# Layer 0's differential attention: the second score product over all 128 rows, with k's halves copied by DMA, and a head's closing transposes one iteration later

## The chip, the cores and the metric

The kernel runs on one core of a Trainium2 chip. The metric is the device time of one execution in microseconds. Differences are judged on repeated executions of both kernels; the profile is one execution of its own.

## The reference

Two encoder layers over 512 tokens of width 1024 are computed in float32. Each layer applies a token mixer, then cross-attention into 256 memory tokens, then a gated MLP, each followed by a layer norm. The mixer of layer 0 is the part that matters here, differential attention with 8 heads. A head has two query and key components of 64 numbers and one value of 128:

```python
s = jnp.einsum('bqhce,bkhce->bhcqk', q_blk, k) * (E ** -0.5)
s = s - slopes[None, :, None, None, None] * dist[None, None, None]
p = jax.nn.softmax(s, axis=-1)
attn = p[:, :, 0] - lam_full * p[:, :, 1]
return jnp.einsum('bhqk,bkhe->bqhe', attn.astype(v.dtype), v)
...
o = rms_norm(o, subln) * (1.0 - lambda_init)
return o.reshape(B, S, D) @ w_o
```

## The kernel before

Almost all matrix products take both operands as a sum of a high and a low part, each in the format float32r: hi is a cast of the number, lo is the rest. `mm3` (lines 238 to 245) issues three products of 512 columns, hi*hi, hi*lo and lo*hi (lines 239, 240, 241), into one PSUM bank. TensorE's order is written out by hand. The orders of the other engines come from a scheduler.

**The heads loop of layer 0** (`diff_attention`, from line 496). `proj(h)` computes a head's q, then its k, each by 24 products into one bank of 128 rows: component 0 in rows 0 to 63, component 1 in rows 64 to 127. `stack_q` (line 468) makes two tiles of 128 rows, q0 with component 0's hi in rows 0 to 63 and its lo in rows 64 to 127, q1 with component 1's hi in rows 64 to 127 and its lo in rows 0 to 63. `stack_k` (line 477) makes k0 and k1, with a component's hi in both halves of the rows, and one tile kl with the lo of component 0 in rows 0 to 63 and that of component 1 in rows 64 to 127. It takes four casts of 64 rows on ScalarE (lines 480, 481, 484, 485) and two subtractions on VectorE (482, 483).

`scores(h, q)` (line 552) handles 128 queries and 512 keys. `stacked_scores` (line 487) issues four products into two banks: a 128-row product for each component, which gives q_hi*k_hi + q_lo*k_hi (line 490), and then for each component a product over 64 rows alone, which adds q_hi*k_lo (line 493). VectorE adds the distance table and takes the extreme (line 561), ScalarE takes the exponential (563), VectorE joins the two components (566 to 568). `turn` (571) transposes the result with four products (574), and ScalarE copies it (576). `values` (579) multiplies by V (582) and normalises: a square on ScalarE (585), a small step on VectorE (586), a power on GpSimd (588, the tile rr), and the tile `on` on VectorE (589, 590). `close` (592) transposes a head's four pieces of `on` (595) and splits them into hi and lo.

`main` (600) runs these as a pipeline over n = 32 iterations, four to a head, and LAG + 2 = 4 more. Iteration i issues scores of i, turn of i - 2, values of i - 3, and behind the values of every fourth iteration the close of the head whose last values came one iteration before. It yields a position ahead of each step. `weave` (287) fills the time up to that position with the products of the next head's `proj`, at head 2 with `vproj1` as well, and at the end with the first output products (`early`). In the additional iterations `take(late, 1900)` issues more output products. `proj(0)` runs ahead of the loop, and then 0.4 of `proj(1)` stands ahead of the first scores.

POOL (GpSimd) issues nothing in the loop but the power of line 588. It issues DMAs of its own in layer 1 alone (line 764 among them, the loads of F). The weights come by SP's queue (line 181), and are split by ScalarE and VectorE (218, 219).

## Time and profile before

| | |
|---|---|
| Three executions | 1897.64, 1899.86, 1900.0 us, median 1899.86 |
| The profiled execution, its own time | 1899.72 us |
| Span of the profile (first to last instruction) | 1897.9 us |
| Granted TensorE clock, mean | 0.998 |
| Busy: TensorE, VectorE, ScalarE, GpSimd | 1871.9, 952.9, 763.3, 73.0 us |
| First and last score product of layer 0 | 45.5 and 223.6 us |

Engines are PE (TensorE's products), PEld (its weight loads, which overlap products), DVE (VectorE), ACT (ScalarE), POOL (GpSimd) and SP (SyncE, which issues DMAs). L490 is line 490 of the kernel. Products are pipelined, so the durations of neighbours overlap, and the distance of two starts says what one costs. A wait's row names the waiting instruction and what released it; "issue" means that nothing in the profile held it. A group's row ends with busy time and mean duration, a timeline's row begins with start and duration.

### The profile page before, as it was taken

Reading aid. Unit: us, or ns where it says so; the run is one execution under the profiler, and the core shown is the slowest. Engines: PE = TensorE matmul, PEld = TensorE weight load, DVE = VectorE, ACT = ScalarE, POOL = GpSimd, SP = SyncE. Lnnn points to the kernel's source line nnn. Section 1 sums busy time; section 2 is a strip of 40 time slices with the busy share of each in tenths; the row PEclk is TensorE's granted clock in tenths of the full one; section 3 lists DMA queues with packets and bytes.
Section 4 is the critical chain, followed back from the end, with each engine's and each line's share of the span. In section 5 each row is a group of like instructions: output and inputs, shape, how many; then the busy total and the mean of one; then the engine's idle time right before and its main releaser. Section 6 shows DMA issues by size and latency. Waiting matters only on the chain.

```text
span 1897.9 us, 25004 instructions
## 1 busy us (share of the span) xinstructions
PE 1871.9 (99%) x9896; PEld 1574.6 (83%) x9896; DVE 952.9 (50%) x1761; ACT 763.3 (40%) x1372; POOL 73.0 (4%) x116
## 2 busy tenths in 40 slices
PE   9999999999999999999999999998999999999998
PEld 7777788889888888898898898987888898888886
DVE  5588675557444432533444344444855564444324
ACT  4567654325333321324434344343544243333211
POOL 0001110000000000000000000001000000000000
PEclk9999999999999999999999999999999999999999
DMA  6121066234332334332322232221651352333241
GB/s 237 45 78 56 23 219 191 67 118 150 100 97 93 100 100 151 104 120 100 97 77 84 78 101 87 80 80 46 224 189 65 122 157 90 99 100 96 93 144 45
DMA packets 61573, 204.35 MB, mean 108 GB/s; under 512 B 8080, under 2 KB 8720, under 8 KB 61456
## 3 DMA queue, kind: packets, MB, share of 16 engines
q1 hardware_dynamic: 46080, 165.89, 27.5%
q10 hardware_dynamic: 12816, 32.47, 4.7%
q0 software_dynamic: 2560, 4.39, 1.0%
q8 instruction: 78, 1.28, 0.3%
q14 instruction: 39, 0.32, 0.1%
HBM read 190.01 MB, written 12.71 MB: 107 GB/s over the span
## 4 chain that ended last, share of the span: by engine, by line
PE 92%; DVE 4%; DMA 2%; ACT 1%; issue 1%; POOL 0%; DVEq 0%; POOLq 0%; ACTq 0%; SPq 0%
PE ps_a L239 17%; PE ps_a L240 16%; PE ps_a L241 16%; PE ps_o L239 7%; PE ps_o L241 7%; PE ps_o L240 7%; PE ps_s L241 2%; PE ps_s L240 2%; PE ps_s L239 2%; PE ps_t L239 2%; PE ps_t L241 2%; PE ps_t L240 2%; PE S L716 1%; PE ps_t L785 1%; PE ps_t L770 1%; PE ps_o L582 1%
## 5 line engine op out<-in xcount | busy, mean ns | idle before, releaser
L219 DVE TENSOR_TENSOR wlo<-raw,whi 128x1024 fp32r<-128x1024 f32 (+1 forms) x309 | 376.7, 1220 | 454.5 <-ACT whi L218 449.3
L218 ACT CAST whi<-raw 128x1024 fp32r<-128x1024 f32 (+1 forms) x309 | 323.6, 1049 | 574.3 <-PE ps_a L240 277.6
L239 PE MATMUL ps_a<-x2h,whi 128*128 128x512 f32 (+1 forms) x384 | 152.4, 397 | 0.0
L241 PE MATMUL ps_a<-x2h,wlo 128*128 128x512 f32 (+1 forms) x384 | 146.6, 382 | 0.0
L240 PE MATMUL ps_a<-x2l,whi 128*128 128x512 f32 (+1 forms) x384 | 146.2, 381 | 0.0
L239 PE MATMUL ps_a<-whi,x2h 128*128 128x512 f32 (+1 forms) x256 | 90.2, 352 | 0.0
L725 DVE CUSTOM_DVE_ANT_0 u<-S,tabd 128x256 f32<-128x256 f32 x128 | 48.8, 420 | 79.0 <-PE ps_t L770 78.2
L240 PE MATMUL ps_a<-wlo,x2h 128*128 128x512 f32 (+1 forms) x256 | 87.1, 340 | 0.0
L241 PE MATMUL ps_a<-whi,x2l 128*128 128x512 f32 (+1 forms) x256 | 87.1, 340 | 0.0
L241 PEld LDWEIGHTS ps_a<-x2h,wlo 128*128 128x128 f32 x384 | 72.2, 188 | 14.5
L239 PEld LDWEIGHTS ps_a<-x2h,whi 128*128 128x128 f32 x384 | 72.3, 188 | 14.3 <-issue 1.5
L727 ACT ACTIVATE u<-u,st 128x256 f32<-128x256 f32 x128 | 64.0, 502 | 47.2 <-DVE st L725 47.0
L240 PEld LDWEIGHTS ps_a<-x2l,whi 128*128 128x128 f32 x384 | 72.5, 189 | 11.6
L239 PE MATMUL ps_o<-x1h,whi 128*128 128x512 f32 (+1 forms) x192 | 71.6, 373 | 0.0
L239 PE MATMUL ps_o<-x4h,whi 128*128 128x512 f32 (+1 forms) x192 | 71.6, 373 | 0.0
L240 PE MATMUL ps_a<-x4l,whi 128*128 128x512 f32 (+1 forms) x192 | 71.3, 372 | 0.0
L239 PE MATMUL ps_a<-x1h,whi 128*128 128x512 f32 (+1 forms) x192 | 71.3, 372 | 0.0
L240 PE MATMUL ps_a<-x1l,whi 128*128 128x512 f32 (+1 forms) x192 | 71.3, 372 | 0.0
L239 PE MATMUL ps_a<-x4h,whi 128*128 128x512 f32 (+1 forms) x192 | 71.3, 371 | 0.0
L241 PE MATMUL ps_a<-x4h,wlo 128*128 128x512 f32 (+1 forms) x192 | 71.3, 371 | 0.0
L241 PE MATMUL ps_a<-x1h,wlo 128*128 128x512 f32 (+1 forms) x192 | 71.3, 371 | 0.0
L241 PE MATMUL ps_o<-x1h,wlo 128*128 128x512 f32 (+1 forms) x192 | 71.3, 371 | 0.0
(420 smaller groups left out, 4487.5 us busy)
## 6 DMA issues: line engine op xcount, KB each, us to landing
raw<-in_wall_dram SPq DMA_DIRECT2D x314, 512.0 KB, 3.5
y<-row ACTq DMA_DIRECT2D x40, 256.0 KB, 3.0
row<-y ACTq DMA_DIRECT2D x20, 512.0 KB, 5.4
row<-in_lngb_dram ACTq DMA_DIRECT2D x12, 512.0 KB, 4.6
F<-fd POOLq DMA_DIRECT2D x16, 256.0 KB, 4.3
row<-in_x_dram ACTq DMA_DIRECT2D x4, 512.0 KB, 6.5
out_dram<-row ACTq DMA_DIRECT2D x8, 256.0 KB, 2.1
raw<-in_wall_dram ACTq DMA_DIRECT2D x2, 256.0 KB, 4.4
```

Source lines behind the costliest of these rows:

```text
L218: nc.scalar.copy(hi, ps)
L219: nc.vector.tensor_tensor(lo, ps, hi.bitcast(F32), op=ALU.subtract)
L239: nc.tensor.matmul(ps, ah, bh, start=start, stop=False)
L240: nc.tensor.matmul(ps, ah, bl, start=False, stop=False)
L241: nc.tensor.matmul(ps, al, bh, start=False, stop=stop)
L582: nc.tensor.matmul(o, PT[:, k, :], V[:, k, sl(h)], start=k == 0, stop=k == 3)
L716: nc.tensor.matmul(Ss[b, c][:, f], q_[h, b, :], k_[h], start=True, stop=True)
L725: nc.vector.tensor_tensor_reduce(out=u[:, f], in0=S[:, f], in1=t, scale=-slope, scalar=3.0e38, op0=ALU.add, op1=ALU.min, accum_out=m)
L727: nc.scalar.activation(u[:, f], u[:, f], AF.Exp, bias=m, scale=-1.0, accum_out=s[:, b, 2 * c + 1:2 * c + 2])
L770: nc.tensor.transpose(tp[:, k, :], u[:, sl(k)], ident)
L785: nc.tensor.matmul(o[sl(c, 64), sl(2 * (n // 2) + x)], V[:, :64], PTs[2 * x + c][:, n, :], start=n % 2 == 0, stop=n % 2 == 1)
```

## The change

Each of k0 and k1 becomes a tile of 128 rows, two planes and 512 columns: a component's hi in plane 0 and its lo in plane 1, both in both halves of the rows. A component's own half is filled by a cast on ScalarE and a subtraction on VectorE, and the other half by one DMA of 64 rows x 4 KB on GpSimd's queue. The tile kl is gone. The second score product of a component takes plane 1 over all 128 rows, so that q_lo*k_lo is added as well, and the four products come component by component. The close of a head moves from the iteration after its last values to the one after that, the loop has one more iteration, and the positions in the last head's stretch are divided accordingly.

```diff
-    def stack_k(ps, k0, k1, kl):
+    def stack_k(ps, k0, k1):
 
         a, b = slice(0, 64), slice(64, 128)
-        nc.scalar.copy(k0[a, :], ps[a, :])
-        nc.scalar.copy(k1[b, :], ps[b, :])
-        nc.vector.tensor_tensor(kl[a, :], ps[a, :], k0[a, :].bitcast(F32), op=ALU.subtract)
-        nc.vector.tensor_tensor(kl[b, :], ps[b, :], k1[b, :].bitcast(F32), op=ALU.subtract)
-        nc.scalar.copy(k0[b, :], ps[a, :])
-        nc.scalar.copy(k1[a, :], ps[b, :])
-
-    def stacked_scores(Ss, t, qs, ks, kl):
-
-        for c, S in enumerate(Ss):
-            nc.tensor.matmul(S, qs[c][:, t], ks[c], start=True, stop=False)
-        for c, S in enumerate(Ss):
-            h = sl(c, 64)
-            nc.tensor.matmul(S, qs[c][h, t], kl[h, :], start=False, stop=True)
+        for k, h, o in ((k0, a, b), (k1, b, a)):
+            nc.scalar.copy(k[h, 0, :], ps[h, :])
+            nc.vector.tensor_tensor(k[h, 1, :], ps[h, :], k[h, 0, :].bitcast(F32), op=ALU.subtract)
+            nc.gpsimd.dma_start(k[o], k[h])
...
-            k = [ap.tile([128, 512], F32R, tag=f"k{c}", name="k") for c in range(3)]
+            k = [ap.tile([128, 2, 512], F32R, tag=f"k{c}", name="k") for c in range(2)]
             stack_k(ps, *k)
-            qk[h] = q, k[:2], k[2]
+            qk[h] = q, k
...
-            stacked_scores(Ss, sl(q), *qk[h])
+            for c, (qc, kc) in enumerate(zip(*qk[h])):
+                for n in range(2):
+                    nc.tensor.matmul(Ss[c], qc[:, sl(q)], kc[:, n, :], start=n == 0, stop=n == 1)
...
-            for i in range(n + LAG + 2):
+            for i in range(n + LAG + 3):
                 seg = min(i // 4, DH - 1)
-                base = (i - 4 * seg) / (4.0 if seg < DH - 1 else LAG + 5.0)
-                step = 1.0 / 12 if seg < DH - 1 else 1.0 / (3 * LAG + 15)
+                base = (i - 4 * seg) / (4.0 if seg < DH - 1 else LAG + 6.0)
+                step = 1.0 / 12 if seg < DH - 1 else 1.0 / (3 * LAG + 18)
...
-                j = i - LAG - 2
+                j = i - LAG - 3
                 if 0 <= j < n and j % 4 == 3:
                     close(j // 4, on.pop(j // 4))
```

In the changed kernel the lines behind `stack_k` have other numbers: the casts are L481, the subtractions L482, the copies L483, the score products L549, turn's products L566, those of values L574 and those of close L587.

TensorE, around the first scores of head 3, before. The values of iteration 11 (L582) are followed by the close of head 1 (L595), a filling product of each kind and the scores (L490, L493):

```order
L582 MATMUL ps_o<-V,PT 128x128 x4
L595 MATMUL ps_t<-ident,on 128x128 x4
L239 MATMUL ps_a<-xh,whi_642 128x512
L240 MATMUL ps_a<-xl,whi_642 128x512
L241 MATMUL ps_a<-xh,wlo_643 128x512
L490 MATMUL ps_s<-k,q 128x512 x2
L493 MATMUL ps_s<-k,q 128x512 x2
```

The same place after. The scores of head 3 (L549, four in one form) follow the values (L574) by three filling products, and the close (L587) stands behind the values of iteration 12:

```order
L574 MATMUL ps_o<-V,PT 128x128 x4
L239 MATMUL ps_a<-xh,whi_639 128x512
L240 MATMUL ps_a<-xl,whi_639 128x512
L241 MATMUL ps_a<-xh,wlo_640 128x512
L549 MATMUL ps_s<-k,q 128x512 x4
```

```order
L574 MATMUL ps_o<-V,PT 128x128 x4
L587 MATMUL ps_t<-ident,on 128x128 x4
L239 MATMUL ps_a<-xh,whi_645 128x512
L240 MATMUL ps_a<-xl,whi_645 128x512
L241 MATMUL ps_a<-xh,wlo_646 128x512
```

So the close has gone from in front of a head's first scores to behind them.

VectorE at head 7's k, before. The names are u and m (scores evacuated, their extreme) and ss (the small step of values); k_2058 is kl:

```order
L568 SCALAR_TENSOR_TENSOR u_2034<-u_2038,rc_2042,u_2034 128x512
L561 ISA u_2099,m_2100<-ps_s_2093,tabf_103 128x512
L561 ISA m_2100 128x1
L482 TENSOR_TENSOR k_2058<-ps_a_1947,k_2056 64x512
L483 TENSOR_TENSOR k_2058<-ps_a_1947,k_2057 64x512
L586 TENSOR_SCALAR ss_2082<-ss_2082 128x1
```

After, k_2049 is k0 and k_2050 is k1:

```order
L560 SCALAR_TENSOR_TENSOR u_2027<-u_2031,rc_2035,u_2027 128x512
L482 TENSOR_TENSOR k_2049<-ps_a_1933,k_2049 64x512
L578 TENSOR_SCALAR ss_2074<-ss_2074 128x1
L553 ISA u_2091,m_2092<-ps_s_2085,tabf_103 128x512
L553 ISA m_2092 128x1
L482 TENSOR_TENSOR k_2050<-ps_a_1933,k_2050 64x512
```

The two subtractions are no longer neighbours: a small step and a score evacuation stand between them. Heads 3 and 5 have the same order.

GpSimd at head 3's k, after. Before, only the powers (rr) stood here:

```order
L580 TENSOR_TENSOR rr_995<-ss_992,mhalf_75 128x1
L580 TENSOR_TENSOR rr_1053<-ss_1050,mhalf_75 128x1
L483 DMA k_1089<-k_1089 64x1024
L483 DMA k_1090<-k_1090 64x1024
L580 TENSOR_TENSOR rr_1119<-ss_1116,mhalf_75 128x1
```

Each copy waits for its component's subtraction, and the next power stands behind both copies.

## The prediction

> **What bounds the kernel now.** I read the page, then the stretch of layer 0's attention, its waits, and the timeline around single score products.

> ```profile
> span 1897.9 us, 25004 instructions
> PE 1871.9 (99%) x9896; PEld 1574.6 (83%) x9896; DVE 952.9 (50%) x1761; ACT 763.3 (40%) x1372; POOL 73.0 (4%) x116
> PE 92%; DVE 4%; DMA 2%; ACT 1%; issue 1%; POOL 0%; DVEq 0%; POOLq 0%; ACTq 0%; SPq 0%
> ```

> ```profile
> 120.00:206.00 86.00, 86.00 (x473) 67.00 (x472) 70.43 (x189) 62.63 (x151) 8.77 (x16) 1.00 0.16 50
> ```

> TensorE is busy for 99% of the span and carries 92% of the chain. In 86 us of the heads loop (second view: PE, PEld, DVE, ACT, POOL, then clock and DMA share) it never rests; VectorE has 70.43 us of work and ScalarE 62.63. So time is won here only by a shorter sequence of TensorE instructions, and every wait put on TensorE is lost in full. DMA has room (0.16).

> The waits of the stretch from 36 to 262 us (engine, line, tile, released by, us in total, times, longest):

> ```profile
> PEld ps_s L493 <- issue: 11.4, 32, 0.4
> PEld ps_a L239 <- issue: 7.2, 30, 0.2
> ...
> PEld ps_s L490 <- DVE m L561: 1.2, 3, 0.5
> ...
> PEld ps_t L595 <- DVE on L590: 0.5, 1, 0.5
> PEld ps_s L490 <- ACT k L485: 0.3, 1, 0.3
> ```

> The two large rows are the weight loader, not held by any engine: once per iteration ahead of the 64-row product (L493), and nearly once per iteration ahead of the first projection product behind it. What TensorE itself loses by that is in the timeline (start, duration):

> ```profile
> 82.65 0.40 PE L241 MATMUL ps_a<-whi,xl 128*128 128x512 f32 x1
> 82.88 0.62 PE L490 MATMUL ps_s<-k,q 128*128 128x512 f32 x2
> 83.43 0.50 PE L493 MATMUL ps_s<-k,q 64*128 64x512 f32 x2
> 83.86 0.50 PE L239 MATMUL ps_a<-whi,xh 128*128 128x512 f32 x1
> 84.19 0.40 PE L240 MATMUL ps_a<-wlo,xh 128*128 128x512 f32 x1
> 84.43 0.40 PE L241 MATMUL ps_a<-whi,xl 128*128 128x512 f32 x1
> ```

> Starts are the measure, since durations overlap. A 128-row product of 512 columns takes 0.23 us from start to start (82.65 to 82.88), entering the scores costs nothing, but the two 128-row products take 0.55 instead of 0.46, the 64-row pair 0.43, and the next projection product 0.33.

> ```profile
> L490 PE MATMUL ps_s<-k,q x64: 387/396/502, 45.5 to 223.1; 128*128 128x512 f32 x64
> L493 PE MATMUL ps_s<-k,q x64: 491/493/501, 46.2 to 223.6; 64*128 64x512 f32 x64
> ```

> One 64-row product lasts 0.49 us, and the pair together 0.50: the two halves of the array run side by side.

> **Scores, 32 iterations.** Before: 82.88 to 84.19, 1.31 us, for four score products and one projection product. After: five 128-row products of one form, 5 x 0.23 = 1.15. That is 0.16 less per iteration, 32 x 0.16 = 5.1 us, all on TensorE's path. The count of products stays. The four are reordered (each bank's two now follow each other), as the projection's three do already.

> The trace shows the idle loader on both sides of the 64-row pair. [...]

> **k's copies.** The change drops two 64-row casts per head on ScalarE, which has idle time, so they count as nothing. It adds two copies of 64 rows x 4 KB (256 KB) per head on POOL's queue. Nearest rows:

> ```profile
> L764 POOL DMA_DIRECT2D F<-fd x16: 532/536/536, 923.9 to 1322.9; - x16
> ```

> ```profile
> DMA to landing us min/median/max: 3.5/4.3/5.9
> ```

> ```profile
> y<-row ACTq DMA_DIRECT2D x40, 256.0 KB, 3.0
> ...
> out_dram<-row ACTq DMA_DIRECT2D x8, 256.0 KB, 2.1
> ```

> F's loads (first two rows: POOL's time, then issue to landing) have the queue, the bytes and the 64 rows, but go in pairs 0.53 us apart that share the DMA engines, and read DRAM. Stores of 256 KB from SBUF take 2.1 and 3.0. I take 3.0, since k's copies are over a microsecond apart and read SBUF; bounds 2.1 and 5.9, with F's median 4.3 as the likelier high case. [...] No run here shows a copy inside SBUF.

> Who waits? By the order, k0's cast, its subtraction, k1's cast and k1's subtraction now follow one another (each waits for the reader of the bank ahead of it), and the second copy is issued last.

> Head 0:

> ```profile
> 41.83 0.58 ACT L480 CAST k<-ps_a 64x512 fp32r<-64x512 f32 x1
> ```

> ```profile
> 41.84 1.23 DVE L219 TENSOR_TENSOR wlo<-raw,whi 128x1024 fp32r<-128x1024 f32 x1 [2.79 <-ACT whi L218]
> 43.10 0.68 DVE L482 TENSOR_TENSOR k<-ps_a,k 64x512 fp32r<-64x512 f32 x1
> 43.81 0.69 DVE L483 TENSOR_TENSOR k<-ps_a,k 64x512 fp32r<-64x512 f32 x1
> ```

> ```profile
> 45.55 0.73 PE L490 MATMUL ps_s<-k,q 128*128 128x512 f32 x2
> ```

> k0's subtraction still runs 43.10 to 43.78; k1's cast to 44.4, its subtraction to 45.2, its copy is issued at 45.25 and lands at 48.3. TensorE comes at 45.55 and wants k1 two products later, 46.0: a stall of 2.3 us (1.4 at 2.1, 3.6 at 4.3, 5.2 at 5.9). The 0.1 us that TensorE loses here before (the row L490 <- ACT k) goes.

> Head 1 has its k finished 9.8 us ahead of its first scores:

> ```profile
> 61.85 0.58 ACT L485 CAST k<-ps_a 64x512 fp32r<-64x512 f32 x1
> ```

> ```profile
> 72.23 0.62 PE L490 MATMUL ps_s<-k,q 128*128 128x512 f32 x2
> ```

> A copy of even 5.9 us is hidden there, and in head 2 too, since all of `vproj1` stands between its k and its scores. Head 3, which stands for heads 3 to 6:

> ```profile
> 121.48 0.58 ACT L480 CAST k<-ps_a 64x512 fp32r<-64x512 f32 x1
> ```

> ```profile
> 121.60 0.75 DVE L568 SCALAR_TENSOR_TENSOR u<-u,rc 128x512 f32<-128x512 f32 x1
> ...
> 124.29 0.69 DVE L561 CUSTOM_DVE_ANT_0 u<-ps_s,tabf 128x512 f32<-128x512 f32 x1
> ...
> 125.60 0.34 DVE L590 SCALAR_TENSOR_TENSOR on<-ps_o,rr,sub 128x128 f32<-128x128 f32 x1
> ```

> ```profile
> 126.60 0.60 PE L595 MATMUL ps_t<-ident,on 128*128 128x128 f32 x4
> ...
> 127.74 0.63 PE L490 MATMUL ps_s<-k,q 128*128 128x512 f32 x2
> ```

> k0's subtraction follows u's (122.35) and ends at 123.05; between it and k1's the order now puts a score evacuation (0.69) and a small step, so k1's ends at about 124.65 and its copy lands at 124.7 + 3.0 = 127.7. TensorE wants it at 127.74 + 0.46 - 0.16 (one iteration's saving) - 0.35 (the closing transposes, 126.60 to 126.96, no longer lie ahead) = 127.69. Just in time, so zero; at 4.3 it is 1.3 us each in heads 3 and 5. In heads 4 and 6 the order has both evacuations ahead of k0's subtraction and the weight cast behind k1's, and by the same durations I estimate k1 about 1.1 us sooner: 0.2 each at 4.3.

> Head 7 comes where iterations are shorter:

> ```profile
> 206.69 0.75 DVE L568 SCALAR_TENSOR_TENSOR u<-u,rc 128x512 f32<-128x512 f32 x1
> ```

> ```profile
> 210.29 0.49 PE L595 MATMUL ps_t<-ident,on 128*128 128x128 f32 x3
> 211.02 0.33 PE L595 MATMUL ps_t<-ident,on 128*128 128x128 f32 x1 [0.23 <-DVE on L590]
> ...
> 211.88 0.62 PE L490 MATMUL ps_s<-k,q 128*128 128x512 f32 x2
> ```

> The same steps from 207.44 end at 209.7, so k1 lands at 212.75. TensorE wants it at 211.88 + 0.46 - 0.16 - 0.81 (transposes with their wait) = 211.37: a stall of 1.4 (0.5 at 2.1, 2.7 at 4.3, 4.3 at 5.9).

> **Closing transposes.** Four transposes move past one iteration; their count stays. What goes is head 5's wait inside them, 0.81 - 0.36 = 0.45 us. What the move covers: pow on POOL now stands behind the second copy.

> ```profile
> 124.34 0.55 POOL L588 TENSOR_TENSOR rr<-ss,mhalf 128x1 f32<-128x1 f32 x1 [6.25 <-DVE ss L586]
> ```

> It would start at 124.7 + 0.53 = 125.25, 0.9 later, and `on` end at 126.85 instead of 125.94. At the old place the fourth transpose, which alone reads this `on`, would stand at about 126.8 (126.60 + 3 x 0.11, less 0.16): 0.1 us of waiting in heads 1 to 4, more with every later copy. An iteration on, there is none. The additional iteration at the end brings no instruction of its own.

> **Sum.** 5.1 + 0.45 + 0.1 = 5.6 us won; 2.3 + 1.4 = 3.7 lost; -1.9. The profiled execution took 1899.72 (0.14 under the median), so 1897.8. A measurement of this kernel can tell about 0.2%, 3.8 us; the three runs lie 2.4 apart.

> **Rivals.**
> - *The copies are hidden.* Landing at 2.1, losses are 1.9: 1896.0; if VectorE and ScalarE also run earlier than I reckon, up to no loss at all, 1894.1. For it: the copies read SBUF and DMA share is 0.16. Against: head 0 has 0.75 us between issue and use.
> - *The copy's landing takes the place of the gain.* At F's 4.3: 3.6 + 2.6 + 0.4 + 2.7 = 9.3 lost, 3.7 net, 1903.4; at 5.9 heads 3 to 7 wait about 2 to 4 each, 1913. It decides from 3.5 on, where losses reach the 5.6. For it: same queue and shape. Against: F's pairs share the engines.
> - *The gaps aren't the 64-row form's.* If 0.09 and 0.10 remain, an iteration costs 1.35, 0.03 more than before, 1 us in all: -0.55 + 3.7 + 1 gives 1903.9. Against: projection products in the same form run without gaps.
> - *Side by side is worth a product.* If the pair's true price is one product, the change adds 32 x 0.23 = 7.4: 1910. [...] Against: the pair takes 0.43, nearly two products' 0.46.
> - *Nothing reaches the end,* a later wait absorbing it: 1899.7. Against: no rest in 120 to 206.

> **How the numbers follow.** My own case (landing 2.5 to 3.5, 1896.8 to 1899.7) 0.48; hidden copies 0.31, of it 0.27 under 1895.9, which is faster by over 0.2%; late copies 0.12, of it 0.10 above 1903.7, slower by over 0.2%; gaps remaining 0.05 (0.04 slower); side by side 0.02; absorbed 0.02. That makes 0.27, 0.57 and 0.16. The range reaches from all copies hidden to F's median.

> **What would show it.** Right: L549 four products 0.23 apart, the next projection product 0.23 behind; loader's issue rows gone; a wait of L549 on k's copies at 46 to 49 and near 212, none at heads 1 and 2, under 0.5 at 3 to 6; no wait at L587 until the last; copies landing near 3. Wrong: landings over 3.5 with a wait at each head, gaps left at the scores, or a wait of L566 or L587 on something behind POOL.

## The result and the profile after

| | before | after |
|---|---|---|
| Median of six executions, us | 1899.39 (1896.87 to 1902.91) | 1908.51 (1906.43 to 1912.74) |
| The profiled execution, its span, us | 1897.9 | 1907.0 |
| Granted TensorE clock, mean of that execution | 0.998 | 0.993 |

The ratio is 1.0052, 95% interval 1.0042 to 1.0062: the change costs 9 to 10 us. The forecast was 1.9 us the other way, and its range ended at F's median, 1903.4.

The page of the changed kernel, span, TensorE and chain:

```profile
span 1907.0 us, 25066 instructions
...
PE 1872.8 (98%) x9896; PEld 1586.9 (83%) x9896; DVE 952.2 (50%) x1761; ACT 756.0 (40%) x1356; POOL 86.3 (5%) x132
...
PE 81%; DVE 3%; DMA 2%; issue 1%; ACT 1%; POOL 0%; DVEq 0%; POOLq 0%; ACTq 0%; SPq 0%
```

TensorE no longer has 92% of the chain. The 86 us of the heads loop in which it never rested (columns PE, PEld, DVE, ACT, POOL, clock, DMA share, GB/s) now hold 3.3 us of rest, at a clock of 0.98, and DMA's share has gone from 0.16 to 0.26:

```profile
120.00:206.00 86.00, 82.67 (x451) 68.96 (x450) 65.99 (x181) 56.97 (x138) 15.26 (x24) 0.98 0.26 68
```

The score products themselves came out as forecast. The same kind of place as the one shown of before, from TensorE's timeline:

```profile
85.83 1.08 PE L549 MATMUL ps_s<-k,q 128*128 128x512 f32 x4
86.74 0.39 PE L239 MATMUL ps_a<-whi,xh 128*128 128x512 f32 x1
86.97 0.39 PE L240 MATMUL ps_a<-wlo,xh 128*128 128x512 f32 x1
```

From 85.83 to 86.97 are 1.14 us for four score products and one of the projection, where it was 1.31. So the loss lies elsewhere, first of all in waits. TensorE's waits between 40 and 230 us (before: two rows of 0.2 us in all of this stretch):

```profile
PE ps_s L549 <- DMA k<-k: 7.2, 6, 2.6
PE ps_a L239 <- DVE k L482: 0.8, 1, 0.8
PE ps_s L549 <- DVE rc L559: 0.8, 1, 0.8
PE ps_s L549 <- DVE m L553: 0.7, 1, 0.7
```

That is 9.5 us, 7.2 of it for the copies. They stand at heads 0 (2.63 us), 3 (1.01 and 0.57), 5 (0.75 and 0.88) and 7 (1.08 and 1.03, and 0.81 of the early output products, whose bank waits for k's last subtraction). The last row, 0.73 us, is a wait of head 6's third scores for an evacuation by VectorE. The 0.75 at head 5 is put down to VectorE's `rc`, which the scores do not read; a copy issued 3.0 us earlier, at 172.24, is the likelier cause. Heads 1, 2, 4 and 6 wait for no copy. Most copies are not slow; the two of head 0 are the longest, 4.1 and 3.8 us. Their issues on POOL (min, median, max in ns, first and last start) and their landing in us:

```profile
L483 POOL DMA_DIRECT2D k<-k x16: 509/514/672, 42.6 to 218.0; - x16
...
DMA to landing us min/median/max: 2.9/3.0/4.1
```

And there is a second loss. The first scores of head 3 in TensorE's timeline:

```profile
128.78 0.40 PE L241 MATMUL ps_a<-xh,wlo 128*128 128x512 f32 x1
130.19 0.70 PE L549 MATMUL ps_s<-k,q 128*128 128x512 f32 x2 [1.01 <-DMA k<-k]
131.47 1.00 PE L549 MATMUL ps_s<-k,q 128*128 128x512 f32 x2 [0.57 <-DMA k<-k]
132.25 0.63 PE L239 MATMUL ps_a<-xh,whi 128*128 128x512 f32 x1
132.68 0.63 PE L240 MATMUL ps_a<-xl,whi 128*128 128x512 f32 x1
```

Behind the wait a product lasts 0.63 instead of 0.40, and the next one starts 0.43 later instead of 0.23. The windows tell why; the column ahead of the DMA share is the granted clock, the first busy time is TensorE's:

```profile
42.95:46.36 3.41, 1.29 (x6) 0.75 (x4) 0.69 (x1) 0.00 (x0) 0.86 (x2) 1.00 0.94 273
46.36:53.19 6.83, 6.32 (x15) 4.64 (x16) 3.39 (x8) 3.76 (x7) 0.00 (x0) 0.50 0.04 8
...
128.28:131.69 3.41, 1.82 (x8) 0.97 (x8) 1.84 (x8) 1.39 (x5) 1.52 (x3) 1.00 0.68 135
131.69:135.10 3.41, 3.41 (x11) 2.74 (x11) 2.31 (x7) 2.47 (x6) 0.10 (x1) 0.50 0.02 5
...
217.03:220.44 3.41, 1.64 (x5) 0.79 (x5) 2.40 (x8) 2.35 (x7) 1.94 (x4) 1.00 0.85 191
220.44:227.26 6.82, 5.86 (x22) 5.32 (x23) 3.30 (x12) 2.67 (x7) 0.36 (x1) 0.50 0.00 0
```

Three stretches of 3.41 us in which TensorE worked for 1.29, 1.82 and 1.64 us are each followed by half clock, for 6.83, 3.41 and 6.82 us. TensorE was busy in those for 6.32 + 3.41 + 5.86 = 15.6 us, and half of that, 7.8 us, is what I estimate that they cost. Before had no such spell here.

The account of this stage in the profiled executions: 9.5 of waits and 7.8 of half clock, less the 5.6 that the forecast had counted as won, make 11.7. The last product ahead of the turning of the rows, before and after:

```profile
264.09 0.39 PE L241 MATMUL ps_o<-whi,o0l 128*128 128x512 f32 x1
```

```profile
275.35 0.39 PE L241 MATMUL ps_o<-whi,o0l 128*128 128x512 f32 x1
```

It comes 11.3 us later, counted from the first instruction. But ahead of the heads the two executions differ as well: the last product ahead of head 0's scores started at 45.31 before and at 43.85 after, so the stage itself grew by 12.7 us. The account falls 1.0 short mostly because of how a wait is counted, from the end of the product ahead, 0.40 us behind its start, while the next product could have started 0.23 behind it. So each wait costs some 0.17 us more than its row says: 1.5 for the nine of after, 0.3 for the two of before.

The span grew by 9.1: 2.2 us came back behind this point, where the code of both kernels is the same. The time from there to the end lay between 1629 and 1634 us in all the traces of this study, and before has the longest, so I take the 2.2 for scatter.

### The profile page after: what moved, and what is told of

It is laid out like the page before. It is cut to its first block, busy times and chain, and to the rows that moved or that the text cites. A ratio compares the mean times of both kernels' runs of the same rounds, so it can differ in the third digit from the quotient of the medians.

```text
span 1907.0 us, 25066 instructions
## 1 busy us (share of the span) xinstructions
PE 1872.8 (98%) x9896; PEld 1586.9 (83%) x9896; DVE 952.2 (50%) x1761; ACT 756.0 (40%) x1356; POOL 86.3 (5%) x132
## 4 chain that ended last, share of the span: by engine, by line
PE 81%; DVE 3%; DMA 2%; issue 1%; ACT 1%; POOL 0%; DVEq 0%; POOLq 0%; ACTq 0%; SPq 0%
PE ps_a L239 15%; PE ps_a L240 14%; PE ps_a L241 14%; PE ps_o L239 7%; PE ps_o L241 7%; PE ps_o L240 7%; PE ps_s L241 2%; PE ps_s L240 2%; PE ps_s L239 2%; PE ps_t L241 2%; PE ps_t L239 2%; PE ps_t L240 2%; PE S L708 1%; PE ps_t L777 1%; PE ps_t L762 1%; DVE wlo L219 1%
## 5 line engine op out<-in xcount | busy, mean ns | idle before, releaser
L219 DVE TENSOR_TENSOR wlo<-raw,whi 128x1024 fp32r<-128x1024 f32 (+1 forms) x309 | 376.9, 1221 | 452.9 <-ACT whi L218 447.8
L218 ACT CAST whi<-raw 128x1024 fp32r<-128x1024 f32 (+1 forms) x309 | 323.3, 1048 | 556.2 <-PE ps_a L240 264.4
L239 PE MATMUL ps_a<-x2h,whi 128*128 128x512 f32 (+1 forms) x384 | 152.5, 397 | 0.0
L241 PE MATMUL ps_a<-x2h,wlo 128*128 128x512 f32 (+1 forms) x384 | 146.7, 382 | 0.0
L240 PE MATMUL ps_a<-x2l,whi 128*128 128x512 f32 (+1 forms) x384 | 146.3, 381 | 0.0
L239 PE MATMUL ps_a<-whi,x2h 128*128 128x512 f32 (+1 forms) x256 | 90.2, 352 | 0.0
L240 PE MATMUL ps_a<-wlo,x2h 128*128 128x512 f32 (+1 forms) x256 | 87.2, 340 | 0.0
L241 PE MATMUL ps_a<-whi,x2l 128*128 128x512 f32 (+1 forms) x256 | 87.1, 340 | 0.0
L241 PEld LDWEIGHTS ps_a<-x2h,wlo 128*128 128x128 f32 x384 | 72.2, 188 | 14.5
L239 PEld LDWEIGHTS ps_a<-x2h,whi 128*128 128x128 f32 x384 | 72.3, 188 | 14.2 <-issue 1.5
L240 PEld LDWEIGHTS ps_a<-x2l,whi 128*128 128x128 f32 x384 | 72.5, 189 | 11.6
L239 PE MATMUL ps_o<-x4h,whi 128*128 128x512 f32 (+1 forms) x192 | 71.7, 373 | 0.0
L239 PE MATMUL ps_o<-x1h,whi 128*128 128x512 f32 (+1 forms) x192 | 71.7, 373 | 0.0
L240 PE MATMUL ps_a<-x4l,whi 128*128 128x512 f32 (+1 forms) x192 | 71.4, 372 | 0.0
L240 PE MATMUL ps_a<-x1l,whi 128*128 128x512 f32 (+1 forms) x192 | 71.4, 372 | 0.0
L241 PE MATMUL ps_a<-x1h,wlo 128*128 128x512 f32 (+1 forms) x192 | 71.4, 372 | 0.0
L239 PE MATMUL ps_a<-x4h,whi 128*128 128x512 f32 (+1 forms) x192 | 71.4, 372 | 0.0
L241 PE MATMUL ps_a<-x4h,wlo 128*128 128x512 f32 (+1 forms) x192 | 71.4, 372 | 0.0
L239 PE MATMUL ps_a<-x1h,whi 128*128 128x512 f32 (+1 forms) x192 | 71.4, 372 | 0.0
L240 PE MATMUL ps_o<-x1l,whi 128*128 128x512 f32 (+1 forms) x192 | 71.4, 372 | 0.0
## 6 DMA issues: line engine op xcount, KB each, us to landing
y<-row ACTq DMA_DIRECT2D x40, 256.0 KB, 2.6
k<-k POOLq DMA_DIRECT2D x16, 256.0 KB, 3.0
F<-fd POOLq DMA_DIRECT2D x16, 256.0 KB, 4.2
out_dram<-row ACTq DMA_DIRECT2D x8, 256.0 KB, 2.0
```

The lines of the kernel that those rows point to most:

```text
L218: nc.scalar.copy(hi, ps)
L219: nc.vector.tensor_tensor(lo, ps, hi.bitcast(F32), op=ALU.subtract)
L239: nc.tensor.matmul(ps, ah, bh, start=start, stop=False)
L240: nc.tensor.matmul(ps, ah, bl, start=False, stop=False)
L241: nc.tensor.matmul(ps, al, bh, start=False, stop=stop)
```

## Experiments

The first theory: k's copies come too late at heads 0, 3, 5 and 7, TensorE waits, and the idle time lowers its clock (T1). Against it: the moved close costs (T2), the copies' traffic costs (T3), the cheaper product brings nothing (T4), the clock has nothing to do with the waits (T5). The kernel before was timed again beside each group of experiments, with medians of 1897.05 (no copies, their traffic, head 0 by the engines, first useless products), 1897.38 (the lead and its control, both on the close alone), 1896.29 (priority, priority with head 0's lead, old close with head 0's lead, second useless products) and 1897.45 (head 0's lead alone, the two more places for the close); the changed kernel at its ratio of 1.0052 would have 1906 to 1907 there. All ratios below are to that kernel before.

**The other halves without copies.**

```diff
-            nc.gpsimd.dma_start(k[o], k[h])
+            nc.scalar.copy(k[o, 0, :], ps[h, :])
+            nc.vector.tensor_tensor(k[o, 1, :], ps[h, :], k[h, 0, :].bitcast(F32), op=ALU.subtract)
```

> The changed kernel, but the other halves of k are filled by two more casts on ScalarE and two more subtractions on VectorE a head, and no copy is issued. T1 (the copies land too late at heads 0, 3, 5 and 7, and the 8.8 us of waits that follow put the granted clock to half for 17 us, which costs another 8.5 us): the cheaper second product stays, waits and half clock go, about 1895 us (1893 to 1898), no half clock between 40 and 230 us. T2 (the moved close and the additional iteration cost the time): as the changed kernel, 1907 to 1910. T4 (the cheaper second product is worth nothing at the end): as the kernel before, 1898 to 1901.

Measured 1907.36, ratio 1.0058 (1.0046 to 1.0071). T1 misses by 12 us; the number is that of T2, but the waits tell another cause. TensorE's, between 40 and 230 us:

```profile
PE ps_a L239 <- DVE k L484: 4.7, 2, 4.3
PE ps_s L550 <- DVE k L484: 3.8, 5, 0.9
PE ps_s L550 <- ACT k L483: 2.5, 5, 1.0
```

11.0 us, and a spell of half clock behind the longest of them. That one, 4.3 us, is of this run's own making: at head 7 the early output products wait for k's bank until the added subtraction has read it. The other two rows, 6.3 us, are waits for k, without any copy. But the added steps, two casts of 0.58 and two subtractions of 0.69 us a head, take 2.5 us themselves, nearly a copy's 3.0. So the run shows that the loss needs no copy, and not whether the landing is late or the steps ahead of it are.

**The copies' traffic alone:** the same, and the copies go on into a tile kd that nothing reads.

```diff
+            nc.gpsimd.dma_start(kd[o], k[h])
```

> The other halves are filled by ScalarE and VectorE as in the first of these kernels, and the copies of the change are issued as well, into a tile that nothing reads: their traffic and GpSimd's work without anyone waiting for them. T1 (the wait is what costs): as the kernel without copies, within 1 us of it, about 1895. T3 (the copies' traffic, or the power standing behind them on GpSimd's queue, costs): 3 us or more above the kernel without copies, up to the changed kernel's 1908.

1908.28, ratio 1.0069 (1.0056 to 1.0081), 0.9 us above the kernel without copies, with the same waits. The level was missed with that kernel's, but the comparison holds: traffic and GpSimd's work cost about 1 us by the medians. With five executions of each a cost of 3 us is not excluded. T3 falls as the main cause all the same, since the kernel without any traffic is as slow as the changed one.

**Head 0 alone filled by the engines** (the two lines above under `if h == 0`, the copy otherwise).

> The changed kernel, with head 0's halves filled by ScalarE and VectorE and all other heads' by the copies. T1 prices head 0's wait at 2.6 us and its spell of half clock at 3.4 us, so about 1902.5 us (1901 to 1904.5), with the spells at heads 3 and 7 still there. If the wait alone costs, 1905.5 to 1906.5; if the copies of head 0 cost nothing, 1908.5.

1906.36, ratio 1.0051 (1.0037 to 1.0065): missed, nothing gained that can be told. Head 0's wait fell to 1.3 us and its half clock went, but the other waits grew, from 6.9 to 7.7 us in all, and the mean clock of the five executions, 0.9952, is the changed kernel's. What TensorE did not wait for at head 0 it partly waited for at later heads.

**Products of no use in the waits**, first with the change as it is.

```diff
+            for n in range({0: 12, 3: 8, 5: 8, 7: 12}.get(h, 0) if q == 0 else 0):
+                nc.tensor.matmul(Ss[0], act[0][:, 0, sl(q)], act[0][:, 0, :], start=True, stop=True)
```

> The changed kernel with products of no use, written to the bank that the scores then start afresh: 12 ahead of the first scores of heads 0 and 7, 8 ahead of those of heads 3 and 5, at 0.229 us each 9.2 us in all, about the 8.8 us that TensorE waits there. The copies land no earlier, so the waits stay, only TensorE is not idle in them. T1 (an idle TensorE lowers the granted clock, and that is 8.5 us of the price): about 1900.5 us (1899 to 1903) with full clock in this stage. T5 (the half clock has nothing to do with the waits): 1908 to 1910, with the half clock there still.

1903.47, ratio 1.0038 (1.0025 to 1.0051), between the two. The waits at heads 3, 5 and 7 were filled, but new ones came up at head 4 (0.85 and 0.84 us, with a spell of 3.41 us behind them) and at head 6 (0.93). Since the waits moved, this settles nothing on the clock; it was tried again below at one head.

**The lead.** More of the next head's projection is issued ahead of a head's first scores: 0.7 of head 1's and 0.6 of those of heads 3 to 7, where it was 0.4. This is done in the changed kernel and, as a control, in the kernel before:

```diff
-(proj(h + 1), 10368 * (3 if h + 1 == V1_AT else 1))
+(proj(h + 1), 10368 * (3 if h + 1 == V1_AT else 1), LEADF if h + 1 == V1_AT else 0.6 if h else 0.7)
```

> The changed kernel, copies and all, with the next head's projection further ahead of the first scores: 0.7 of head 1's projection before head 0's scores, 0.6 ahead at the others (0.4 before, and still at head 2), so k's copies start some 3 us earlier for head 0 and 4 us earlier for the others. Nothing else is changed. T1 (k is ready too late for the first scores, whether the copies or the engines fill it): no waits for k at heads 0, 3, 5, no half clock there, the cheaper second product stays: 1892 to 1896 where the kernel before has 1897. T2 (the moved close costs): 1905 to 1908.

> The kernel before with the same lead as the run above, as its control. T1: the kernel before waits 0.45 us in all at its close and its scores, so a longer lead brings nothing: the same within 1 us, or a little slower where a stretch without filling products is left behind head 0. If the lead brought 3 us or more here, a gain of the run above would not be the copies'.

The changed kernel took 1898.84, ratio 1.0012 (1.0003 to 1.0021), the control 1902.18, ratio 1.0025 (1.0015 to 1.0036). With the lead the changed kernel has no wait for a copy and no half clock in this stage, but both kernels now wait at their scores for the evacuation of earlier ones, 5.0 and 4.0 us by their waits. The expected level was missed by that. Beside its control the changed kernel is 3.3 us faster: with k in time the cheaper product does reach the end, and T4 falls.

**The close alone.** The kernel before with the move of the close, its additional iteration and positions (the change's lines in `main`, nothing else), and the changed kernel without them.

> The kernel before with nothing of the change but the close an iteration later, the additional iteration and the positions of the last stretch. T1: within 1.5 us of the kernel before. T2: 4 us or more slower.

> The changed kernel with the close at its old place, ahead of a head's first scores, and no additional iteration. T1: the close's four transposes give the copies 0.4 us more of cover at heads 3, 5 and 7, so each wait there is that much shorter, and if a wait falls below what lowers the clock, 1.7 us more with it: 1902 to 1908. T2: as the kernel before, or faster, 1893 to 1898.

Alone, the move is free: 1896.25, ratio 0.9994 (0.9986 to 1.0003). The changed kernel without it takes 1899.06, ratio 1.0007 (0.9999 to 1.0016). That lies between the two forecasts and meets neither. So T2 is wrong as it stood, and yet 8 us hang on the move: it costs only together with the rest of the change. The waits with the old close:

```profile
PE ps_t L587 <- DVE on L582: 2.9, 4, 1.8
PE ps_s L549 <- DMA k<-k: 2.8, 1, 2.8
```

One wait for a copy is left, head 0's. At heads 4 to 7 the close itself waits for `on`. The run led to a new theory, T6: the moved close set the steps of VectorE and ScalarE later against the scores, and uncovered copies that would have been covered.

**Priority for k's steps**, with the change as it is.

```diff
-            stack_k(ps, *k)
+            with tc.high_priority(offset=URGENT):
+                stack_k(ps, *k)
```

> The changed kernel, moved close and copies as they are, but the casts, subtractions and copies of k get a higher priority in the scheduler, so on ScalarE a head's first cast of k stands ahead of the exponentials and the copy of PT at heads 3, 5 and 7, where it stood behind them. T6 (the moved close only put k's casts later in ScalarE's and VectorE's order, by 2 to 3 us against the scores, and so uncovered copies that were covered before): the waits at heads 3, 5 and 7 go, and the half clock there, head 0's 2.6 us and its half clock stay: 1896 to 1899. If the copies are late whatever the order: 1905 to 1908.

1904.6, ratio 1.0045 (1.0032 to 1.0058): missed. ScalarE did cast earlier, VectorE followed only in part. Head 3, ScalarE and VectorE:

```profile
119.81 0.57 ACT L481 CAST k<-ps_a 64x512 fp32r<-64x512 f32 x1
```

```profile
121.76 1.22 DVE L219 TENSOR_TENSOR wlo<-raw,whi 128x1024 fp32r<-128x1024 f32 x1
122.89 0.68 DVE L482 TENSOR_TENSOR k<-ps_a,k 64x512 fp32r<-64x512 f32 x1
```

The cast was done at 120.4. The subtraction starts at 122.89, behind two evacuations and a weight split of 1.22 us, and k1 follows k0. Measured against the scores one iteration ahead of the head, k1's subtraction ended 3.1 us behind at head 3 instead of 3.8, but at heads 4 and 6 it came later than in the changed kernel (3.1 and 2.4 instead of 1.0 and 1.6). TensorE waited at heads 3 to 7, each, and the copies' median landing was 3.9 us in this kernel, 0.9 longer, so that the run does not test the order alone.

**Head 0's lead alone,** 0.7 of head 1's projection ahead and all other heads at 0.4: with the old close, with the priority, and with nothing else.

```diff
-(proj(h + 1), 10368 * (3 if h + 1 == V1_AT else 1))
+(proj(h + 1), 10368 * (3 if h + 1 == V1_AT else 1), LEADF if h else 0.7)
```

> The changed kernel with the close at its old place, and 0.7 instead of 0.4 of head 1's projection ahead of head 0's first scores, the other heads as they were. The run with the old close took 1899.1 with a wait of 2.8 us at head 0 and 6.8 us of half clock there, 3.4 us lost. T6: both go, 0.5 us comes back as a wait behind head 0: 1892.5 to 1895. If head 0's wait is paid elsewhere later: 1898 to 1900.

> The changed kernel with both, the higher priority for k's steps and the longer lead at head 0; the moved close stays. T6: no wait for k at any head and no half clock in this stage, the close waits for nothing: the cheaper second product is left alone, 1890.5 to 1893.5, faster than the kernel before by 4 to 7 us. If the moved close costs by itself, 1896 or more.

> The changed kernel with the longer lead at head 0 alone; the moved close stays, and the order at heads 3, 5 and 7 is the changed kernel's. T1 and T6: head 0's wait of 2.6 us and its half clock (up to 3.4 us) go, heads 3, 5 and 7 still wait 1.6, 1.6 and 2.9 us: 1900.5 to 1903.5 where the changed kernel has 1906. If head 0's loss only comes back later: 1905 to 1907.

With the old close 1896.16, ratio 0.9993 (0.9984 to 1.0002), a little over the expected range. Its waits:

```profile
PE ps_t L587 <- DVE on L582: 3.0, 4, 1.8
PE ps_s L549 <- DVE m L553: 0.3, 1, 0.3
```

No copy is waited for, but the close's wait takes 3.0 of the 5.1 us won. With the priority 1901.51, ratio 1.0027 (1.0018 to 1.0036), missed like the priority alone. With nothing else 1902.59, ratio 1.0027 (1.0017 to 1.0036), as expected: head 0 is worth nearly 5 us, heads 3, 5 and 7 keep their waits.

**One more try at the clock,** at head 0 with the old close, where one wait stands by itself.

```diff
+            for n in range(11 if h == q == 0 else 0):
+                nc.tensor.matmul(Ss[0], act[0][:, 0, sl(q)], act[0][:, 0, :], start=True, stop=True)
```

> The run with the close at its old place (1899.1), with 11 products of no use ahead of head 0's first scores, 2.5 us, in the wait of 2.8 us that TensorE has there. The copies land no earlier. T1 (an idle TensorE lowers the granted clock): the wait stays, the 6.8 us of half clock go, 3.4 us less: 1895 to 1897. T5 (the clock does not follow from the wait): 1899 to 1900, half clock there still.

TensorE at the first scores with the old close, without and with the useless products (L548), and the windows of both:

```profile
48.67 2.21 PE L549 MATMUL ps_s<-k,q 128*128 128x512 f32 x4 [2.78 <-DMA k<-k]
```

```profile
44.97 2.65 PE L548 MATMUL ps_s<-xh 128*128 128x512 f32 x11
...
48.67 0.70 PE L551 MATMUL ps_s<-k,q 128*128 128x512 f32 x2 [0.34 <-DMA k<-k]
```

```profile
48.14:54.97 6.83, 6.30 (x15) 4.70 (x16) 3.40 (x8) 3.76 (x7) 0.00 (x0) 0.50 0.04 7
```

```profile
40.00:60.00 20.00, 19.65 (x88) 15.68 (x87) 12.07 (x27) 10.49 (x21) 1.69 (x3) 1.00 0.26 80
```

The useless products fill the wait, the second pair still stands 0.34 us for its copy behind them, and the half clock is gone. In the medians it is not settled: 1897.21, ratio 1.0004 (0.9995 to 1.0013), against 1.0007 (0.9999 to 1.0016) without the useless products, where 3 us were expected. By the mean clocks, 0.9969 with the useless products and 0.9963 without, at most about 1 us came back. So in the average execution the spell seems to cost less than the 3.4 us of the profiled one.

**Two more places for the close,** both with head 0's lead: with a filling position ahead of the old place, and directly behind the next head's first scores.

```diff
                     values(j // 4, j % 4, *PT.pop(j), on[j // 4])
+                yield seg + base + 2.7 * step
                 j = i - LAG - 2
```

> The run with the old close and the longer lead at head 0 (1896.2), with one filling position between the values and the close. On ScalarE k's first cast stands between the two exponentials at heads 3 to 7, as in that run. T6 (the order around k's steps decides): no wait for k at any head; the 3.0 us that the close waited for on at heads 4 to 7 fall to 1 to 1.8 us: 1893.5 to 1895.5 where the kernel before has 1896.3, so faster than both kernels. If it gives nothing: 1896 to 1897.

```diff
                 if i < n:
                     P[i] = scores(i // 4, i % 4)
...
+                j = i - LAG - 3
+                if 0 <= j < n and j % 4 == 3:
+                    close(j // 4, on.pop(j // 4))
                 yield seg + base + step
```

The same three lines further down go.

> The changed kernel with the longer lead at head 0 and the close directly behind the next head's first scores, half an iteration earlier than in the change. By its order k's first cast stands behind both exponentials and the copy of PT at heads 3 to 7, at all five, and k's second subtraction behind a weight split. T6: TensorE waits for k at heads 3 to 7, 1 to 2 us at each, 5 to 9 us in all: 1899 to 1903. If the order does not matter (the copies cover themselves, or the place of the close alone decides): no such waits, 1892 to 1895.

The first took 1896.26, ratio 0.9994 (0.9985 to 1.0002), over the expected range: no wait for k, as expected, but the position put no product ahead of the close at heads 4 to 6, and its waits there stayed at 0.29, 0.46 and 0.48. At head 7 the close's wait fell from 1.76 to 1.03, and a wait of 0.88 at head 7's scores came up in its place. The second took 1903.33, ratio 1.0031 (1.0018 to 1.0043), 0.3 us over T6's range, with a wait at each of the five heads, as T6 expected:

```profile
PE ps_s L549 <- DMA k<-k: 8.4, 5, 3.1
PE ps_s L549 <- DVE m L553: 0.5, 1, 0.5
```

No version was faster than the kernel before by more than its interval. The two with the old close and head 0's lead beat the changed kernel by about 11 us.

An account over the runs that have the cheaper product and no useless ones. From the profiled execution it takes TensorE's waits between 40 and 230 us with their number, and half of TensorE's busy time at half clock up to the turning of the rows. The account is waits + 0.17 us for each + half clock - 5.9, where 5.9 is 5.1 for the cheaper product and 0.8 for the two waits of before. Beside it stands by how much the stage was longer than before in the same trace, from TensorE's 131st product, in head 0's projection, to the last one ahead of the turning. The last column is the difference measured over all executions (ratio less 1, times 1900). All times are in us.

| kernel | waits | half clock | account | stage in the trace | measured |
|---|---|---|---|---|---|
| the changed kernel | 9.5 (9) | 7.8 | +12.9 | +12.7 | +9.9 |
| no copies | 11.0 (12) | 2.5 | +9.7 | +9.7 | +11.0 |
| no copies, their traffic | 11.0 (12) | 2.4 | +9.6 | +10.2 | +13.1 |
| head 0 by engines | 9.0 (11) | 3.0 | +8.0 | +8.2 | +9.7 |
| old close | 5.7 (5) | 3.1 | +3.8 | +4.3 | +1.3 |
| lead at all heads | 5.0 (6) | 0 | +0.1 | +1.6 | +2.3 |
| priority | 9.7 (12) | 0 | +5.8 | +6.4 | +8.5 |
| priority, lead at head 0 | 6.8 (10) | 1.6 | +4.2 | +5.1 | +5.1 |
| old close, lead at head 0 | 3.3 (5) | 0 | -1.7 | -1.4 | -1.3 |
| same, filling position | 3.5 (6) | 0 | -1.4 | -0.9 | -1.1 |
| lead at head 0 | 8.0 (10) | 0 | +3.8 | +4.2 | +5.1 |
| close behind scores | 8.9 (6) | 4.4 | +8.5 | +8.7 | +5.9 |

In the traces waits and half clock give the stage to within 0.9 us, 1.5 with the lead at all heads. Part of the rest is that the product behind a wait holds the next one for 0.31 us instead of 0.23 (head 3). The measured differences lie up to 3 us to either side of the stage in the one traced execution.

## Why the prediction was wrong, step by step

**Scores: right.** 1.14 us for 1.15, and the 0.09 us ahead of the 64-row pair (0.55 less 0.46) and 0.10 behind it (0.33 less 0.23) are gone with the 64-row form. That side by side is worth a product is out.

**Copies' landing: right, but for head 0.** Median 3.0 as taken, 2.9 to 4.1 in this kernel. Head 0's two copies took 4.1 and 3.8, in a stretch with a DMA share of 0.94, where the forecast had read room from the loop's mean of 0.16. The rival that made the landing late is not what happened at the other heads.

**Head 0: the size right, by luck.** 2.3 forecast, 2.63 measured:

```profile
46.87 2.24 PE L549 MATMUL ps_s<-k,q 128*128 128x512 f32 x4 [2.63 <-DMA k<-k]
```

The forecast had TensorE wait for k1, two products in, with a landing of 3.0. It waited for k0, ahead of the first product, with a landing of 4.1, and no wait for k1 shows behind it, since the two products ahead of that ran at half clock (0.50 from 46.36 to 53.19). By the forecast's own working a landing of 4.3 would have cost 3.6.

**Heads 3 to 6, "Just in time, so zero": this step failed.** It placed k's subtractions by VectorE's times of before, and took TensorE alone to move. In TensorE's timelines the scores of the iteration ahead of head 3 start at 122.08 before and 124.01 after, and k1 is wanted 5.6 us behind them, as reckoned (127.69 - 122.08) and as it came (130.19 - 1.01 + 0.46 - 124.01). But k1's subtraction, reckoned to end 2.6 us behind those scores (124.65 - 122.08), ended 3.8 behind (127.77 - 124.01). The two scores, before and after:

```profile
122.08 0.63 PE L490 MATMUL ps_s<-k,q 128*128 128x512 f32 x2
```

```profile
124.01 1.08 PE L549 MATMUL ps_s<-k,q 128*128 128x512 f32 x4
```

VectorE and POOL at head 3 after:

```profile
125.03 0.75 DVE L560 SCALAR_TENSOR_TENSOR u<-u,rc 128x512 f32<-128x512 f32 x1
125.70 0.68 DVE L482 TENSOR_TENSOR k<-ps_a,k 64x512 fp32r<-64x512 f32 x1
...
127.08 0.69 DVE L482 TENSOR_TENSOR k<-ps_a,k 64x512 fp32r<-64x512 f32 x1
```

```profile
126.92 0.56 POOL L483 DMA_DIRECT2D k<-k  x1 [5.06 <-DVE ss L578]
128.31 0.51 POOL L483 DMA_DIRECT2D k<-k  x1 [0.83 <-issue]
```

POOL starts the copy 0.54 us behind the end of the subtraction, where the forecast had 0.05. 1.2 and 0.5 make 1.7; head 3 waits 1.6.

Why VectorE is late stands two iterations ahead of those scores. There, with the close now in the first iteration of head 2, TensorE issues the second iteration's scores at 113.87, and VectorE has this ahead of their evacuation:

```profile
115.25 1.22 DVE L219 TENSOR_TENSOR wlo<-raw,whi 128x1024 fp32r<-128x1024 f32 x1
116.91 0.16 DVE L581 TENSOR_TENSOR rr<-rr,rc 128x1 f32<-128x1 f32 x1 [0.44 <-POOL rr L580]
117.10 0.69 DVE L219 TENSOR_TENSOR o0l<-ps_t,o0h 128x512 fp32r<-128x512 f32 x1
117.71 0.34 DVE L582 SCALAR_TENSOR_TENSOR on<-ps_o,rr,sub 128x128 f32<-128x128 f32 x1
117.97 0.68 DVE L553 CUSTOM_DVE_ANT_0 u<-ps_s,tabf 128x512 f32<-128x512 f32 x1
```

A weight split, a wait for the power, the close's own subtraction and `on`: the evacuation starts 4.1 us behind its scores. In the kernel before it was 2.2, 113.90 behind 111.67 (VectorE, then TensorE):

```profile
113.90 0.69 DVE L561 CUSTOM_DVE_ANT_0 u<-ps_s,tabf 128x512 f32<-128x512 f32 x1
```

```profile
111.67 0.63 PE L490 MATMUL ps_s<-k,q 128*128 128x512 f32 x2
```

In the changed kernel the same five rows stand in the same order at heads 4 and 6, with 4.6 and 5.2 us, and the heads behind these, 3, 5 and 7, are the ones that wait. Behind head 3's wait VectorE has caught up (scores at 138.13, evacuation at 139.10, the split done at 135.6), and head 4 is in time; so it goes at 5 and 6. That the close's place decides is shown by the runs (old close: no wait for k at heads 3 to 7; close behind the scores: a wait at all five); that it does so through this order in the changed kernel is read from the traces. The close alone does not make this order: in the kernel before with the moved close the same evacuation starts 2.5 us behind its scores. Nor is it the only order that does harm: with the close behind the scores it starts 2.0 behind, and k's steps are late all the same.

What the runs have in common is when k is done. The table has, in us, by how much k1's subtraction ended behind the start of the scores one iteration ahead of the head, and the heads among these five at whose first scores TensorE had to wait. The priority with head 0's lead is like the priority, and the other runs with the old close are like the old close.

| kernel | head 3 | head 4 | head 5 | head 6 | head 7 | waits at |
|---|---|---|---|---|---|---|
| the changed kernel | 3.8 | 1.0 | 3.8 | 1.6 | 4.5 | 3, 5, 7 |
| lead at head 0 | 3.8 | 1.7 | 3.8 | 1.6 | 4.5 | 3, 5, 7 |
| head 0 by engines | 3.8 | 1.7 | 3.8 | 1.7 | 4.5 | 3, 5, 7 |
| priority | 3.1 | 3.1 | 3.1 | 2.4 | 3.7 | all five |
| close behind scores | 3.2 | 2.4 | 2.5 | 2.5 | 3.2 | all five |
| old close | 1.1 | 1.8 | 2.0 | 2.0 | 2.7 | none |
| lead at all heads | -1.8 | -1.0 | -1.0 | -1.0 | 1.3 | none |

Wherever the subtraction ended 2.4 us or more behind, TensorE waited; wherever it ended 2.0 or less behind, it did not. The one exception, 2.7 at head 7 with the old close, is covered by the 1.75 us that the close itself waits for `on` there.

**Head 7: right in kind, half the size.** 1.4 forecast, 1.08 + 1.03 and 0.81 for the bank measured, for the same reason (4.5 in the table).

**Closing transposes: the gain was there, its price was not seen.** The close waits for nothing after, and the 0.45 is won. The forecast counted only what the close leaves on TensorE and POOL, and not that its evacuation and what the scheduler sets around it go into VectorE's queue ahead of the next evacuations.

**The waits in all.** The forecast had 3.7 us, 9.5 were measured: 0.3 more at head 0, 3.2 at heads 3 and 5, 1.5 more at head 7, and 0.7 at head 6 for the late evacuation.

**The clock was not in the sum at all.** Every wait was priced at its length. In the profiled execution half clock cost 7.8 us more, by the estimate above. Over all six executions of the changed kernel the mean clock was 0.995, against 0.9972 to 0.9977 for the kernel before. If 0.001 of the clock costs 0.001 of the time, 1.9 us, that is 4 to 5 us of the 9. The executions say less: compared within each kernel, over all 230 whose clock was taken, a mean clock lower by 0.001 went with 0.8 us more, give or take 0.3, which makes it about 2 us. Two things in the traces fit that. The mean takes in the end of the span, which runs at half clock with TensorE idle: the last 3.7 us before and the last 7.2 after. And TensorE waited less for later copies where it had run at half clock: 6.9 us at heads 3 to 7 in the changed kernel, and 7.7 in the run with the lead at head 0, whose trace has no half clock in this stage.

The spells in this stage last 3.41 or 6.83 us, and their starts in this execution, 46.36, 131.69 and 220.44, lie 85.33 and 88.75 us apart, 25 and 26 times 3.413. In none of the three did TensorE stand still through the whole 3.41 us ahead: ahead of the second (128.28 to 131.69) it worked for 1.82 us, and half clock followed.

What stays open is how much of the 9 us an average execution loses to the clock, between 2 and 5: both runs made for it left it unsettled in the medians.

## What to carry to other kernels

When an edit makes the bounding engine faster or moves work to another place in its order, reckon the other engines' steps anew against it: their times of before are no dates, and a cover that is as long as the latency is no cover. An edit that is harmless alone can cost together with another, so try each without the other. A wait on a busy TensorE is to be priced at its length and, where half clock follows it in the trace, at up to half of that spell, which in this stage was 3.41 to 6.83 us long.

## What was not expected of the hardware

```profile
115.42 1.46 POOL L580 TENSOR_TENSOR rr<-ss,mhalf 128x1 f32<-128x1 f32 x1 [6.13 <-DVE ss L578]
```

- A copy of 256 KB inside SBUF landed in 2.8 us at the least (second useless products); the kernels' medians go from 2.9 to 3.9 (this in both with the priority), the longest took 5.2, in the kernel with the close behind the scores, in a stretch in which DMA moved 203 GB/s. What decides is open.
